# Hybrid decoder trunk: A's heads moved to the output projection, top-k rounds spread, side work ahead of weight splits, B turned a step earlier

## The chip, the cores and the metric

The kernel runs on one core of a Trainium2 chip. The metric is the device time of one execution in microseconds, given as the median of several runs.

## What is computed

Two layers of a decoder trunk, batch 1, 256 positions, model width 1024, all in float32:

```
h = h + 1/2 * SwiGLU_1(RMSNorm(h))
u = RMSNorm(h);  P = u @ W_in          # 3792 columns: A q,k,v | index q,k,w | B q,k,v | C q,k,v,f,g
o_A = sparse attention: 4 query heads, one shared key/value head; keys chosen per query by an
      indexer: score = sum_h w_h * relu(iq_h . ik), causal, the top 64 of 256
o_B = 4 heads; at 256 positions one block, so plain causal attention
o_C = 8 heads with a cumulative log-forget bias and a sigmoid gate
h = h + concat(o_A, o_B, o_C) @ W_out
h = h + 1/2 * SwiGLU_2(RMSNorm(h))
```

A and B use normalised and rotated queries and keys, C normalised ones.

## The kernel before

**Weights.** All large products run with the weights as two rounded halves (high and low), three matmuls for one (`mm3`). Each weight unit (128 x up to 1024) is split on the chip: ScalarE casts it to the high half (line 116), VectorE subtracts to get the low half (line 120). `W.take()` hands out the next unit; `W.pump()` queues one cast, and one subtraction for the unit before, as long as fewer than seven units are split ahead. There are eight buffers of split units and five raw 1 MB buffers, filled by SyncE's DMA queue.

**Order.** Every engine runs its instructions in the order in which the program issues them; there is no scheduler. Tiles rotate through pools: a new tile waits until the readers of the tile that had its place are done. PSUM has two rotating sets of four banks, `gu` and `acc`.

**The mixer.** First the input projection: eight chunks of columns (`CHUNKS`: iq, ib, b, a, ck, cq, cv, cg), four weight units each, so 32 steps. After each step the kernel issues `W.pump()`, counts the step and then issues the *side work* that is due (`at_step`, `run_side`): what has to be done to chunks that are there already, while TensorE goes on with the projections. After a chunk's fourth step its `post_` function evacuates its banks (two `gu` banks for each chunk). The side work, by step:

- 7 to 10: index queries and keys, stacked as high and low halves (`stack`, lines 605 and 606) and turned (`queries_T`, `keys_T`: matmuls with the identity into `acc` banks; ScalarE copies the high half, line 616 or 628, VectorE makes the low half of keys, line 629).
- 11 to 16: `index`: products, ReLU (ScalarE, line 717), weighted sum into `score` (VectorE, line 721).
- 13: `log_sigmoid` (ScalarE, with table loads), `bk_norm` (B's key norm; GpSimd writes the scaled keys twice, line 824). 14: `bq_split`.
- 16 to 23: `topk`, eight rounds that take out the eight largest of each row (VectorE, lines 739 and 741). 24: `amask`.
- 16: `cumsum`: matmul into an `acc` bank, which VectorE reads with four small copies (lines 763 and 764).
- `B_TURN` = 19: `bq_turn` and `bk_turn`, which take two `acc` banks each. From `B_STEP` = 20: B's heads by `run_heads`, one a step.
- 20: `a_norm`, `a_split`. `A_TURN` = 24: `a_turn`. From `A_STEP` = 25: A's heads.
- 21 and 25: C's sums of squares and norm.

`run_heads` makes five stages for a head: `scores` (TensorE; then VectorE scales, masks and takes the row's extreme, line 910), `exps` (ScalarE, lines 917 and 918), `flip` (three transposes, line 924, and a copy to SBUF, line 926; in the output projection by VectorE for even heads, ScalarE for odd ones), `values` (TensorE, then VectorE divides, line 940, and scales into `o`), and `outT` for each pair of heads (two transposes, line 957, then a high half by ScalarE, line 964, and a low half by VectorE, line 965).

**The output projection.** It runs into all four `acc` banks. `out_halves` issues the first five units (k-tiles of `W_out` in the order 2, 3, 0, 1, 4: B's two pairs, A's two, C's first) as ten halves of twelve matmuls, one half for each `next(halves)`, with a `W.pump()` behind each second half. C's eight heads run between the halves in the `gu` banks, software-pipelined: iteration i issues `scores(i)`, `flip(i - 1)`, `exps(i)`, a half, `values(i - 1)`. `c_T` turns two of C's heads (eight transposes, line 1024, two copies, line 1025). `tail` does the last three units, the residual and the next norm.

The two feed-forward blocks of a layer (`ffn`) are outside the change.

Of the kernel before, what the change touches and what calls it, by code (L numbers as in the profile page):

```python
# [35 lines left out]
DOWN_LAG = 4  # L36
OUT_TAIL = 3
WARM = 7
B_TURN, B_STEP, A_TURN, A_STEP = 19, 20, 24, 25


CHUNKS = [
# [9 lines left out]
OUT_ORDER = [2, 3, 0, 1, 4, 5, 6, 7]  # L52
# [88 lines left out]
def kernel(ctx: ExitStack, tc: tile.TileContext, x, ffn1_norm, ffn1_w_gate, ffn1_w_up, ffn1_w_down,  # L141
# [62 lines left out]
    W = Weights(tc, raw_pool, split_pool)  # L204
# [343 lines left out]
    def mixer(l, norm, nxt):  # L548
# [3 lines left out]
        def at_step(n, fn):  # L552
            side.append((n, next(count), fn))

        def run_side():
            due = sorted(x for x in side if x[0] <= step[0])
            for x in due:
                x[2]()
            side[:] = [x for x in side if x[0] > step[0]]
# [98 lines left out]
        def post_ib(ps):  # L658
# [92 lines left out]
                st["amask"] = am  # L751

            for r in range(TOPK // 8):
                at_step(16 + r, topk)
            at_step(24, amask)

            def cumsum():
                b = bank("acc")
# [8 lines left out]
        def post_a(ps):  # L767
            ss = sm.tile([P, 2, 5], F32, name="ssa", tag="ss")
            rot = [hp.tile([P, S], F32, name="aqr", tag="hl") for _ in range(2)]
            ak = [at.tile([P, 1, HD], F32, name=f"ak{t}", tag=f"ak{t}") for t in range(2)]  # L770
            akd = [at.tile([P, 2, HD], F32, name=f"akd{t}", tag=f"kd{t}") for t in range(2)]
            sq = []
            for t in range(2):
                evac(rot[t], ps[t][:, :256], t)
                evac(ak[t][:, 0], ps[t][:, 256:320], t)
                evac(va[t][:, 0, 0:64], ps[t][:, 320:384], t)
                sq.append(squares(ps[t][:, :320], t, 5))
                rope(heads(rot[t], 4), tab[:, 0, 0, t], tab[:, 0, 1, t])
                rope(ak[t], tab[:, 1, 0, t], tab[:, 1, 1, t])

            def a_norm():
                for t in range(2):
                    square_sums(ss[:, t], sq[t])
                rs = head_rs(ss.rearrange("p t h -> p (t h)"), 10, "a")
                for t in range(2):
                    scale_heads(akd[t], ak[t], rs[:, 5 * t + 4:5 * t + 5])
                st["ra"] = minus(rs, 10, "a")

            at_step(20, a_norm)

            def a_split():
                st["aq"] = [stack(x) for x in rot]

            def a_turn():
                st["aqT"] = at.tile([P, 4, S], F32R, name="aqT", tag="qs")
                st["akT"] = at.tile([P, 2, 1, S], F32R, name="akT", tag="ikT")
                queries_T(st["aqT"], st["aq"])
                keys_T(st["akT"], [d.rearrange("p a b -> p (a b)")[:, None] for d in akd])

            at_step(20, a_split)  # L800
            at_step(A_TURN, a_turn)

            def qk_a(h):
                return st["aqT"][:, h], [st["akT"][:, c, 0] for c in range(2)]

            run_heads([("A", h) for h in range(4)], qk_a, "acc", lambda i, fn: at_step(A_STEP + i, fn), 2)

        def post_b(ps):
            ss = sm.tile([P, 2, 4], F32, name="ssbk", tag="ss")
            rot = [hp.tile([P, S], F32, name="bkr", tag="hl") for _ in range(2)]  # L810
            sq = []
            for t in range(2):
                evac(rot[t], ps[t][:, :256], t)
                evac(va[t][:, 1:5, 0:64], heads(ps[t][:, 256:512], 4), t)
                sq.append(squares(ps[t][:, :256], t, 4))
                rope(heads(rot[t], 4), tab[:, 3, 0, t], tab[:, 3, 1, t])

            def bk_norm():
                for t in range(2):
                    square_sums(ss[:, t], sq[t])  # L820
                rs = head_rs(ss.rearrange("p t h -> p (t h)"), 8, "bk")
                for t in range(2):
                    twice = tmp(512).rearrange("p (h s d) -> p h s d", h=4, s=2)
                    G.tensor_tensor(twice, heads(rot[t], 4)[:, :, None, :].to_broadcast([P, 4, 2, HD]),
                                    rs[:, 4 * t:4 * t + 4, None, None].to_broadcast([P, 4, 2, HD]), op=ALU.mult)
                    bk.append(twice.rearrange("p h s d -> p h (s d)"))

            def bk_turn():
                st["bkT"] = at.tile([P, 2, 4, S], F32R, name="bkT", tag="kT")
                keys_T(st["bkT"], bk)  # L830

            bk = []
            at_step(13, bk_norm)
            at_step(B_TURN, bk_turn)

            def qk_b(h):
                return st["bqT"][:, h], [st["bkT"][:, c, h] for c in range(2)]

            run_heads([("B", h) for h in range(4)], qk_b, "acc", lambda i, fn: at_step(B_STEP + i, fn), 2)
# [48 lines left out]
        def run_heads(hs, qk, tag, emit=None, lag=1):  # L888
            pj, pt, op = {}, {}, {}

            def scores(i):

                kind, h = hs[i]
                q, k = qk(h)
                b = bank(tag)
                if kind == "C":
                    mm(b[:, 0:P], q[:, 0:P], k[:, 0:P], True, True)
                    mm(b[:, P:3 * P], q[:, P:S], k[:, 0:S], False, True)
                else:
                    products(b[:, 0:P], q[:, 0:P], [c[:, 0:P] for c in k], True, True)  # L900
                    products(b[:, P:3 * P], q[:, P:S], [c[:, 0:S] for c in k], False, True)
                mask = st["amask"] if kind == "A" else causal
                s = tmp(3 * P)
                nm = sm.tile([P, 2], F32, name="nm", tag="nm")
                for t, c in enumerate((slice(0, P), slice(P, 3 * P))):
                    scale = -1.0
                    if kind != "C":
                        col = (5 * t if kind == "A" else 4 * t) + h
                        scale = st["r" + kind.lower()][:, col:col + 1]
                    V.tensor_tensor_reduce(s[:, c], b[:, c], mask[:, c], scale, 3e38, op0=ALU.add, op1=ALU.min,  # L910
                                           accum_out=nm[:, t:t + 1])
                pj[i] = (s, nm)
# [66 lines left out]
        for name, cols in CHUNKS:  # L979
            n = sum(c[1] for c in cols)  # L980
            ps = [bank("gu") for _ in range(2)]
            for u in range(4):
                w = W.take()
                for kk in range(2):
                    k = 2 * u + kk
                    for t in range(2):
                        ts = slice(t * P, (t + 1) * P)
                        mm3(ps[t][:, :n], (norm.h[:, k, ts], norm.l[:, k, ts]), [v[:, kk] for v in w],
                            k == 0, k == KT - 1)
                if name == "iq" and u == 1:  # L990
                    norm.sums()
                W.pump(2 if name == "iq" else 1)
                step[0] += 1
                run_side()
            posts[name](ps)
        while side:
            step[0] += 1
# [21 lines left out]
        def c_T(hp_):  # L1019
            for d, src in zip(cT, (cqa, cka)):  # L1020
                b = bank("gu")
                for i in range(2):
                    for t in range(2):
                        T.transpose(b[:66, i * S + t * P:i * S + (t + 1) * P], src[t][:, 2 * hp_ + i, :], ident)  # L1024
                (A.copy if src is cqa else V.tensor_copy)(d[:66, 2 * hp_:2 * hp_ + 2],
                                                         b[:66].rearrange("p (a b) -> p a b", a=2))

        scores, exps, flip, values, outT = run_heads([("C", h) for h in range(8)],
                                                     lambda h: (cT[0][:66, h], cT[1][:66, h]), "gu")
        c_T(0)  # L1030
        next(halves)
        for i in range(9):
            if i < 8:
                scores(i)
            if i > 0:
                flip(i - 1)
            if i < 8:
                exps(i)
            if i > 0:
                next(halves)  # L1040
                values(i - 1)
                if i > 2 and i % 2:
                    outT((i - 3) // 2)
            if i in (0, 2, 4):
                c_T(1 + i // 2)
            if i == 0:
                next(halves)
        for _ in halves:
            raise AssertionError
        return tail(acc, oT, OUT_ORDER[8 - OUT_TAIL:], 1.0, nxt, lambda: outT(3))  # L1050


    def before_mixer(l):
# [119 lines left out]
```

## Time and profile before

| | us |
|---|---|
| median of 3 runs | 1066.82 |
| lowest to highest | 1066.6 to 1068.17 |
| the profiled execution | 1066.12 |
| its span, from the first to the last instruction | 1064.3 |

The profile is of one execution. A row of its timeline has the start and the length in us from the span's start, the engine (PE is TensorE, PEld its weight loads, DVE VectorE, ACT ScalarE, POOL GpSimd), the line of the kernel, the operation, what is written and read, the shapes and the number of merged instructions; in brackets the idle time before it and what ended that. TensorE's matmuls overlap, so the time that one costs is the distance between starts. Layer 0's mixer lies at about 198 to 350 us, layer 1's at about 724 to 877 us.

### The profile page before, as it was taken

Reading aid. Unit: us, or ns where it says so; the run is one execution under the profiler, and the core shown is the slowest. Engines: PE = TensorE matmul, PEld = TensorE weight load, DVE = VectorE, ACT = ScalarE, POOL = GpSimd, SP = SyncE. Lnnn points to the kernel's source line nnn. Section 1 sums busy time; section 2 is a strip of 40 time slices with the busy share of each in tenths; the row PEclk is TensorE's granted clock in tenths of the full one; section 3 lists DMA queues with packets and bytes.
Section 4 is the critical chain, followed back from the end, with each engine's and each line's share of the span. In section 5 each row is a group of like instructions: output and inputs, shape, how many; then the busy total and the mean of one; then the engine's idle time right before and its main releaser. Section 6 shows DMA issues by size and latency. Waiting matters only on the chain.

```text
span 1064.3 us, 16903 instructions
## 1 busy us (share of the span) xinstructions
PE 1049.6 (99%) x6611; PEld 950.2 (89%) x6611; DVE 827.4 (78%) x1564; ACT 595.8 (56%) x1022; POOL 160.6 (15%) x184
## 2 busy tenths in 40 slices
PE   9999999998999999999999999999989999999998
PEld 8999999997899899999989999999868998888887
DVE  6998777789856887777789777778897669877774
ACT  6565554676654565555456555547756455655551
POOL 2004000276400100000010300003765000000000
PEclk9999999999999999999999999999999999999999
DMA  9576465464332365564646565464544314564531
GB/s 324 203 240 205 157 231 158 135 222 159 120 118 81 119 237 175 182 207 149 199 159 219 175 208 184 172 185 165 173 148 155 119 41 147 210 234 155 205 119 40
DMA packets 130912, 181.81 MB, mean 171 GB/s; under 512 B 7008, under 2 KB 104720, under 8 KB 130832
## 3 DMA queue, kind: packets, MB, share of 16 engines
q1 hardware_dynamic: 130512, 180.65, 50.4%
q8 instruction: 52, 0.85, 0.3%
q14 instruction: 28, 0.23, 0.1%
q10 hardware_dynamic: 320, 0.08, 0.0%
HBM read 179.67 MB, written 1.05 MB: 170 GB/s over the span
## 4 chain that ended last, share of the span: by engine, by line
PE 59%; DVE 4%; ACT 1%; issue 1%; POOL 1%; POOLq 0%; ACTq 0%; DVEq 0%
PE ps_gu L293 38%; PE ps_acc L293 21%; DVE wl L120 1%; DVE score L721 1%; DVE score L741 0%; PE ps_gu L1024 0%; DVE m L739 0%; PE ps_gu L924 0%; DVE xhl L320 0%; PE ps_acc L924 0%; DVE hres L352 0%; DVE stacked L606 0%; ACT xhl L317 0%; POOL swapped L570 0%; PE ps_acc L383 0%
## 5 line engine op out<-in xcount | busy, mean ns | idle before, releaser
L120 DVE TENSOR_TENSOR wl<-raw,wh 128x1024 fp32r<-128x1024 f32 (+2 forms) x343 | 414.6, 1215 | 22.1 <-ACT wh L116 22.0
L293 PE MATMUL ps_gu<-xhl,wh 128*128 128x512 f32 (+1 forms) x1408 | 351.8, 391 | 0.2 <-DVE tmp L425 0.2
L116 ACT CAST wh<-raw 128x1024 fp32r<-128x1024 f32 (+2 forms) x343 | 345.1, 1035 | 4.0 <-PE ps_gu L293 2.0
L293 PEld LDWEIGHTS ps_gu<-xhl,wh 128*128 128x128 f32 x1408 | 253.6, 189 | 46.2 <-DVE tmp L425 0.4
L293 PEld LDWEIGHTS ps_gu<-xhl,wl 128*128 128x128 f32 x1400 | 192.0, 190 | 13.7
L293 PE MATMUL ps_gu<-xhl,wl 128*128 128x256 f32 x1400 | 198.0, 283 | 0.0
L293 PE MATMUL ps_gu<-wh,xhl 128*128 128x512 f32 (+2 forms) x512 | 162.4, 384 | 0.0
L425 DVE TENSOR_TENSOR tmp<-ps_gu,tmp 128x256 f32<-128x256 f32 x175 | 74.2, 424 | 105.8 <-ACT tmp L424 105.6
L293 PE MATMUL ps_acc<-hl,wh 128*128 128x256 f32 x528 | 149.7, 284 | 0.0
L293 PE MATMUL ps_acc<-hh,wl 128*128 128x256 f32 x528 | 149.4, 283 | 0.0
L293 PE MATMUL ps_acc<-hh,wh 128*128 128x256 f32 x528 | 149.4, 283 | 0.0
L424 ACT COPY tmp<-ps_gu 128x256 f32<-128x256 f32 x175 | 64.7, 370 | 132.7 <-PE ps_gu L293 127.0
L293 PEld LDWEIGHTS ps_gu<-wh,xhl 128*128 128x128 f32 x512 | 96.3, 191 | 14.8
L293 PEld LDWEIGHTS ps_acc<-hl,wh 128*128 128x128 f32 x528 | 101.4, 192 | 0.3
L293 PEld LDWEIGHTS ps_acc<-hh,wl 128*128 128x128 f32 x528 | 101.3, 192 | 0.0
L293 PEld LDWEIGHTS ps_acc<-hh,wh 128*128 128x128 f32 x528 | 101.3, 192 | 0.0
L293 PE MATMUL ps_gu<-wl,xhl 128*128 128x512 f32 (+2 forms) x256 | 96.8, 378 | 0.0
L331 POOL TENSOR_TENSOR ssacc<-ssacc,tmp 128x512 f32<-128x512 f32 x10 | 12.9, 1294 | 506.3 <-ACT tmp L329 327.7
L432 ACT ACTIVATE tmp<-tmp 128x256 f32<-128x256 f32 x88 | 36.8, 418 | 85.3 <-DVE tmp L430 85.3
L441 ACT CAST hh<-tmp 128x256 fp32r<-128x256 f32 x80 | 32.6, 407 | 86.5 <-DVE tmp L437 86.5
L293 PEld LDWEIGHTS ps_gu<-wl,xhl 128*128 128x128 f32 x256 | 49.0, 191 | 6.6
L430 DVE TENSOR_TENSOR tmp<-tmp,rb 128x256 f32<-128x256 f32 x88 | 37.7, 428 | 3.0
(246 smaller groups left out, 1229.9 us busy)
## 6 DMA issues: line engine op xcount, KB each, us to landing
raw<-in_ffn_w_down_dram SPq DMA_DIRECT2D x44, 1024.0 KB, 7.0
raw<-in_ffn_w_gate_dram SPq DMA_DIRECT2D x43, 1024.0 KB, 7.0
raw<-in_ffn_w_up_dram SPq DMA_DIRECT2D x43, 1024.0 KB, 5.2
raw<-in_w_in_dram SPq DMA_DIRECT2D x24, 1024.0 KB, 5.1
raw<-in_w_out_dram SPq DMA_DIRECT2D x8, 1024.0 KB, 4.9
raw<-in_w_in_dram SPq DMA_DIRECT2D x4, 768.0 KB, 5.2
raw<-in_w_in_dram SPq DMA_DIRECT2D x4, 656.0 KB, 4.6
xin<-in_x_dram SPq DMA_DIRECT2D x4, 256.0 KB, 5.2
```

What stands on the lines that cost most here:

```text
L116: self.nc.scalar.copy(hv, src)
L120: (engine or self.nc.vector).tensor_tensor(lv, self.srcs[self.n_low], hv.bitcast(F32), op=ALU.subtract)
L293: T.matmul(o, l, r, start=start, stop=stop, skip_group_check=True)
L331: G.tensor_tensor(self.acc, self.acc, sq, op=ALU.add)
L424: A.copy(o, ps[:, 1])
L425: V.tensor_tensor(o, ps[:, 0], o, op=ALU.add)
L430: V.tensor_tensor(t_, t_, norm.rb, op=ALU.mult)
L432: A.activation(th, t_, AF.Tanh, scale=0.5)
L441: (V.tensor_copy if late else A.copy)(hh, t_)
L721: V.scalar_tensor_tensor(sc, rl[:, i * n:(i + 1) * n], st["iw"][:, t, h:h + 1], st["cmask"][t] if first else sc, op0=ALU.mult, op1=ALU.add)
```

## The change

- A's four heads leave the side work. They become heads 0 to 3 of the list that runs among the halves of the output projection, ahead of C's eight: 13 iterations instead of 9, in the `gu` banks. The ten halves are placed as follows: one ahead of the loop, one in each iteration but 3, 5, 9 and 12. `c_T` runs in iterations 3, 5, 7 and 9 (before: one ahead of the loop, then 0, 2 and 4).
- The eight top-k rounds are due at steps 17, 19, ... 31, and `amask` at 32.
- `B_TURN` is 18 in place of 19; B's heads still start at step 20.
- `a_norm` is due at 22, `a_split` at 24, `a_turn` at 26.
- In each step of the input projection the side work is issued ahead of `W.pump()`, not behind it.

```diff
-B_TURN, B_STEP, A_TURN, A_STEP = 19, 20, 24, 25
+B_TURN, B_STEP, A_ROOT, A_TURN = 18, 20, 22, 26
...
-                at_step(16 + r, topk)
-            at_step(24, amask)
+                at_step(17 + 2 * r, topk)
+            at_step(32, amask)
...
-            at_step(20, a_norm)
+            at_step(A_ROOT, a_norm)
...
-            at_step(20, a_split)
+            at_step(A_TURN - 2, a_split)
             at_step(A_TURN, a_turn)
 
-            def qk_a(h):
-                return st["aqT"][:, h], [st["akT"][:, c, 0] for c in range(2)]
-
-            run_heads([("A", h) for h in range(4)], qk_a, "acc", lambda i, fn: at_step(A_STEP + i, fn), 2)
...
-                W.pump(2 if name == "iq" else 1)
                 step[0] += 1
                 run_side()
+                W.pump(2 if name == "iq" else 1)
             posts[name](ps)
...
-        scores, exps, flip, values, outT = run_heads([("C", h) for h in range(8)],
-                                                     lambda h: (cT[0][:66, h], cT[1][:66, h]), "gu")
-        c_T(0)
+        def qk_ac(kind, h):
+            if kind == "A":
+                return st["aqT"][:, h], [st["akT"][:, c, 0] for c in range(2)]
+            return cT[0][:66, h], cT[1][:66, h]
+
+        hs = [("A", h) for h in range(4)] + [("C", h) for h in range(8)]
+        scores, exps, flip, values, outT = run_heads(hs, qk_ac, "gu")
+        n = len(hs)
         next(halves)
-        for i in range(9):
-            if i < 8:
+        for i in range(n + 1):
+            if i < n:
                 scores(i)
             if i > 0:
                 flip(i - 1)
-            if i < 8:
+            if i < n:
                 exps(i)
+            if i in (3, 5, 7, 9):
+                c_T((i - 3) // 2)
+            if i not in (3, 5, 9, n):
+                next(halves)
             if i > 0:
-                next(halves)
                 values(i - 1)
                 if i > 2 and i % 2:
                     outT((i - 3) // 2)
-            if i in (0, 2, 4):
-                c_T(1 + i // 2)
-            if i == 0:
-                next(halves)
...
-        return tail(acc, oT, OUT_ORDER[8 - OUT_TAIL:], 1.0, nxt, lambda: outT(3))
+        return tail(acc, oT, OUT_ORDER[8 - OUT_TAIL:], 1.0, nxt, lambda: outT(n // 2 - 1))
```

More of the change, by code (lines that the diff above doesn't have):

```diff
@@ L834, in post_b, with qk_b @@
             at_step(B_TURN, bk_turn)
-            def qk_b(h):
+            def qk_b(kind, h):
                 return st["bqT"][:, h], [st["bkT"][:, c, h] for c in range(2)]
@@ L893, in scores @@
                 kind, h = hs[i]
-                q, k = qk(h)
+                q, k = qk(kind, h)
                 b = bank(tag)
```

## The prediction

> **What bounds the kernel now.** I read the page's busy shares first, then TensorE's waits, then the timeline around the longest wait, engine by engine.
>
> ```profile
> PE 1049.6 (99%) x6611; PEld 950.2 (89%) x6611; DVE 827.4 (78%) x1564; ACT 595.8 (56%) x1022; POOL 160.6 (15%) x184
> ```
>
> TensorE is the limit, and the change leaves its matmuls as they are. So a gain can only come out of TensorE's idle time and slow stretches, and a loss only from new ones. TensorE's waits name where they are:
>
> ```profile
> PE ps_acc L293 <- DVE bkT L629: 8.3, 2, 4.1
> ```
>
> Two waits of 4.1 us, one in each layer's mixer, on VectorE's low half of B's turned keys (`keys_T`, line 629). The other waits of TensorE are 1 us or less. The place in layer 0 (the work of step 19, then step 20, then B's first scores, then step 21):
>
> ```profile
> 250.71 1.00 PE L293 MATMUL ps_acc<-identr,stacked 128*128 128x128 f32 x8
> 251.56 1.23 PE L626 MATMUL ps_acc<-cst,tmp 128*128 128x128 f32 x8
> 252.54 0.48 PE L293 MATMUL ps_gu<-wh,xhl 128*128 128x512 f32 x1
> ```
>
> ```profile
> 255.39 0.22 PE L293 MATMUL ps_acc<-bkT,bqT 128*128 128x128 f32 x1
> 259.75 0.76 PE L293 MATMUL ps_acc<-bkT,bqT 128*128 128x128 f32 x3 [4.13 <-DVE bkT L629]
> 260.30 0.63 PE L293 MATMUL ps_gu<-wh,xhl 128*128 128x512 f32 x1
> ```
>
> ```profile
> 264.54 0.62 PE L293 MATMUL ps_acc<-bkT,bqT 128*128 128x128 f32 x4
> 265.00 0.39 PE L293 MATMUL ps_gu<-wh,xhl 128*128 128x512 f32 x1
> ```
>
> Undisturbed, one B score takes 265.00 - 264.54 = 0.46 us and a step of projections behind side work 255.39 - 252.54 = 2.85 us. From 255.39 to 264.54 stand one of each, 3.31 us, and 9.15 us went by: 5.84 us lost, more than the wait. The rest is the clock:
>
> ```profile
> 253.23:256.64 3.41, 2.38 (x12) 1.74 (x10) 3.41 (x14) 1.13 (x2) 3.25 (x5) 1.00 0.14 37
> 256.64:260.06 3.42, 0.31 (x2) 0.31 (x3) 3.42 (x9) 0.00 (x0) 2.23 (x5) 1.00 0.85 302
> 260.06:263.47 3.41, 3.41 (x11) 2.74 (x10) 3.41 (x13) 1.74 (x5) 0.00 (x0) 0.50 0.26 49
> ```
>
> The columns are busy us of PE, PEld, DVE, ACT and POOL, then the granted clock. After a stretch in which TensorE was busy for 0.31 us, the next 3.41 us ran at clock 0.50; after one with 1.03 us idle (2.38 of 3.41 busy) the clock stayed 1.00. Layer 1 is the same:
>
> ```profile
> 781.76 0.22 PE L293 MATMUL ps_acc<-bkT,bqT 128*128 128x128 f32 x1
> ```
>
> ```profile
> 790.69 0.62 PE L293 MATMUL ps_acc<-bkT,bqT 128*128 128x128 f32 x4
> ```
>
> 8.93 us for 3.31: 5.62 us lost. Together 11.46 us are to be had.
>
> VectorE is the late one: it ran without a gap from here
>
> ```profile
> 239.56 0.48 DVE L721 SCALAR_TENSOR_TENSOR score<-tmp,iw,causal 128x256 f32<-128x256 f32 x1 [1.29 <-ACT tmp L717]
> ```
>
> to the keys' low half, and step 16's last index product, made at 241.63, was scored at 248.97:
>
> ```profile
> 241.63 0.63 PE L293 MATMUL ps_acc<-ikT,iqT 128*128 128x256 f32 x4
> ```
>
> ```profile
> 248.97 1.56 DVE L721 SCALAR_TENSOR_TENSOR score<-tmp,iw,score 128x256 f32<-128x256 f32 x2
> 250.46 0.61 DVE L739 MAX8 m<-score 128x8 f32<-128x128 f32 x2
> ```
>
> ```profile
> 251.64 0.15 DVE L763 COPY cqa<-ps_acc 128x8 f32<-128x8 f32 x1
> ...
> 251.93 1.21 DVE L120 TENSOR_TENSOR wl<-raw,wh 128x1024 fp32r<-128x1024 f32 x1
> ```
>
> ```profile
> 259.02 1.27 DVE L629 TENSOR_TENSOR bkT<-ps_acc,bkT 128x512 fp32r<-128x512 f32 x2
> ```
>
> A top-k round is 251.64 - 250.46 = 1.18 us, the cumulative sum's four copies about 0.3, a low split about 1.2.
>
> **The change part by part.** *B turned at step 18, rounds spread.* ScalarE gates the restart at 239.56: VectorE waits there for its ReLU, which stands behind the log-sigmoid's table loads. In the changed order one weight cast that stood between B's evacuations and that chain goes behind it, and the one of the step before goes ahead of the evacuations: the same number of casts ahead of the chain, so I keep 239.56. From there to the end of the scores (250.46) VectorE's order is unchanged. Then the cumulative sum's copies come at once, without the round ahead of them: done at 250.46 + 0.37 = 250.83. Then a split (1.2), one round (1.18), a split (1.2), the keys (1.2): ready at 255.6, not 260.2; four rounds before the keys become one, six splits five.
>
> TensorE now turns B one step earlier. Three steps lie between 242.46 and 250.71, so 2.75 each:
>
> ```profile
> 242.46 0.48 PE L293 MATMUL ps_gu<-wh,xhl 128*128 128x512 f32 x1
> ```
>
> The turn starts at 250.71 - 2.75 = 247.96. Its keys need GpSimd's doubled keys, ready in time at 244.16 + 3.20 = 247.36:
>
> ```profile
> 244.16 3.20 POOL L824 TENSOR_TENSOR tmp<-bkr,y_bk 128x512 f32<-128x512 f32 x2
> ```
>
> But the turn takes four accumulator banks of four, and the last is the one that the cumulative sum's copies read. That wait is already there, small: the fifth key transpose, due 251.56 + 4 x 0.11 = 252.0, came at
>
> ```profile
> 252.16 0.30 PE L626 MATMUL ps_acc<-cst,tmp 128*128 128x128 f32 x1
> ```
>
> 0.15 us after the last copy. After the change TensorE is there at 247.96 + 0.85 + 0.44 = 249.25 and the copies end at 250.83, so it goes on at about 250.95: **a new wait of 1.7 us** in place of 0.15, or +1.55. Behind it: TensorE needs the keys after step 20, at 250.95 + 0.5 + 2.75 + 2.85 = 257.05, and they are ready at 255.6. So the 4.1 us wait goes, with 1.4 us to spare, and with it the half clock.
>
> Can 1.7 us of idleness halve the clock? The rows bound it: 1.03 idle did not, 3.1 did; 1.7 is nearer the first, so I take no loss, with a rival below. The Trainium skill (TensorE: Matmul & The Clock Gate, "What's actually happening") has half rate come after an idle window of some 3.4 us, which a 1.7 us wait cannot fill; by that rule too the sum stays. The trace agrees only loosely, as the window ahead of the half clock still held 0.31 us of work.
>
> *Side work ahead of splits.* The first turn of the index queries waited for a stacked low half behind a split, in both layers, and took 0.39 us longer than the second:
>
> ```profile
> 219.31 1.39 PE L293 MATMUL ps_acc<-identr,stacked 128*128 128x128 f32 x8
> ```
>
> ```profile
> 745.53 1.39 PE L293 MATMUL ps_acc<-identr,stacked 128*128 128x128 f32 x8
> ```
>
> ```profile
> 223.37 1.00 PE L293 MATMUL ps_acc<-identr,stacked 128*128 128x128 f32 x8
> ```
>
> ```profile
> 218.78 0.87 DVE L606 TENSOR_TENSOR stacked<-iqr,stacked 128x256 fp32r<-128x256 f32 x2
> ```
>
> A split now stands behind these two, so they end about 1 us earlier: -0.39 per layer. ScalarE's casts queue behind its ReLUs, which wait for TensorE; weights are split up to seven units ahead, so a step's delay there reaches nobody.
>
> *A's heads moved.* TensorE's work for them is the same. A step of projections behind side work costs 2.85, one without 2.75; steps with side work of TensorE that a projection follows fall from 13 (19 to 31) to 9: -0.4 per layer. A's norm and turn (22, 24, 26) only have to be done by step 32.
>
> *Output projection.* There are 13 iterations for ten halves of 1.5 us, so four (3, 5, 9 and the last, 12) have none. In 3, 5 and 9 the value product waits for VectorE's copy of the turned probabilities. The row of before: scores end at 313.97, the copy ends at 314.73 + 0.55 = 315.28,
>
> ```profile
> 313.97 0.49 PE L924 MATMUL ps_gu<-cst,p 128*128 128x128 f32 x3
> ```
>
> ```profile
> 314.73 0.55 DVE L926 COPY pT<-ps_gu 128x384 f32<-128x384 f32 x1
> ```
>
> 1.31 later, 1.4 with the release. TensorE then has the flip (0.24) and `c_T` (four and four transposes, 0.44 each) to do, 1.12:
>
> ```profile
> 319.43 0.60 PE L1024 MATMUL ps_gu<-cst,cqa 128*66 128x128 f32 x4
> 319.87 0.60 PE L1024 MATMUL ps_gu<-cst,cka 128*66 128x128 f32 x4
> ```
>
> 0.3 us of waiting, three times: +0.9. In the last iteration nothing stands between flip and values:
>
> ```profile
> 337.06 0.49 PE L924 MATMUL ps_gu<-cst,p 128*128 128x128 f32 x3
> 337.30 0.36 PE L293 MATMUL ps_acc<-oh,wh 128*128 128x256 f32 x1
> ```
>
> ```profile
> 337.64 0.48 ACT L926 COPY pT<-ps_gu 128x384 f32<-128x384 f32 x1
> ```
>
> The copy ends at 338.12, so values start at 338.2, 0.9 after the flip: +0.9. Elsewhere a half covers the chain.
>
> **The sum.** Layer 0: -5.84 - 0.39 - 0.4 + 1.55 + 0.9 + 0.9 = -3.28. Layer 1: -5.62 and the same others: -3.06. Together -6.3. The profiled execution took 1066.12 (span 1064.3), the median of the runs is 1066.82, 0.7 above it. I predict against the median: 1066.82 - 6.3 = **1060.5 us**.
>
> **The rivals.**
> 1. *The new wait halves the clock.* Idle of 1.7 lies between the 1.03 and 3.1 of the rows, so it can. Of layer 0's 5.84 us, 260.30 - 255.39 - 0.46 = 4.45 is the wait and 1.4 the clock; twice 1.4: 1063.3. Chance 0.11.
> 2. *The bank wait is not there*, because the copies come sooner: -3.4 more, 1057.1. Against it: the same release gap stands in both layers. Chance 0.07.
> 3. *The 4.1 us wait shortens only*: VectorE is later than I have it by over 1.4 us (two scores that take 1 us took 2.4 while GpSimd doubled the keys). At 4 us later, 2.6 us of waiting come back per layer: 1065.7, no change. Chance 0.06.
> 4. *Slower: VectorE late at the seam.* Four rounds and A's mask now stand in steps 25 to 32, ahead of A's first scores. TensorE reaches A's first flip one half and one score (1.97 us) after the scores, and the chain to it needs about 1.45, so a lag over 0.5 us stalls it. A lag of 7 us is on record at step 16. With 4 us, 3.5 of waiting and 1.4 of clock per layer: 1070.3. It turns into a loss from a lag of about 2.3. Against it is the load there:
>
> ```profile
> 280.00:296.00 16.00, 16.00 (x96) 14.05 (x95) 9.86 (x31) 9.99 (x20) 13.68 (x7) 1.00 0.48 157
> 296.00:308.00 12.00, 12.00 (x68) 10.19 (x68) 6.47 (x13) 6.60 (x10) 0.00 (x0) 1.00 0.30 90
> 308.00:345.00 37.00, 37.00 (x311) 36.17 (x310) 24.50 (x79) 18.20 (x38) 0.00 (x0) 1.00 0.27 86
> ```
>
> VectorE was busy for 9.9 of 16 us and 6.5 of 12, with A's softmax in it; four rounds add 4.7 to the 28 us. Chance 0.06.
> 5. *Transposes leave the clock idle.* Iterations 3, 5 and 9 hold 1.3 us of transposes and 0.3 of waiting in about 2.4 us. If transposes count as idle, each could halve one stretch, at most 1.7 us, six times: 1070.7, slower. Against it, `c_T` and flips stood in 308 to 345 at clock 1.00. Chance 0.03. The Trainium skill (same page, "Part 4: PE-mode transpose") says that transposes do not count as busy in the same way.
>
> **How the numbers follow.** My forecast has 0.64, the rivals 0.33, and 0.03 is left to others. Its own spread is 1058.5 to 1063, as its small terms are each uncertain by half. The range of 1057.0 to 1065.0 takes in the first two rivals; the seam, the transposes and most of rival 3 lie outside. About 0.2% (2.1 us) is what a measurement of this kernel can tell from no change. Faster: the forecast, rivals 1 and 2 and part of 3, 0.86; same 0.06; slower 0.08.
>
> **What would show it.** In the changed profile TensorE's wait for bkT is gone and a wait of 1 to 2.5 us stands among B's key transposes, released by the copies of line 763; clock 1.00 throughout both mixers; waits of 0.2 to 0.5 us ahead of three value products and near 0.9 ahead of the last; A's first flip not late. A wait for the mask or at B's first scores, or a stretch at 0.50, proves me wrong.

## The result, and the profile after

The changed kernel takes **1060.86 us** (median of four runs, 1060.17 to 1061.7) against 1066.94 beside it (four runs, 1066.6 to 1068.17): ratio 0.9941, 95% interval 0.9924 to 0.9958, some 6.1 us less. The profiled execution of the changed kernel took 1061.49 us, with a span of 1059.7. In its profile the line numbers behind `run_heads` are four lower: scores L906, exponentials L913 and L914, flip L920, the copy `pT` L922, `c_T` L1020.

The page's busy shares, and TensorE's waits (us in total, times, longest):

```profile
PE 1049.7 (99%) x6611; PEld 950.5 (90%) x6611; DVE 829.2 (78%) x1568; ACT 594.1 (56%) x1018; POOL 164.1 (15%) x184
```

```profile
PE ps_acc L626 <- DVE cka L764: 3.2, 2, 1.6
PE ps_gu L293 <- ACT pT L922: 1.2, 2, 0.6
PE ps_gu L293 <- POOL minus_half L182: 1.0, 1, 1.0
```

TensorE's busy time is what it was (1049.6). The two waits of 4.1 us for bkT are gone; in their place stand two of 1.6 us for the copies of the cumulative sum (line 764), and one of 0.6 us in each layer for the last turned probabilities. The place in layer 0, TensorE's timeline:

```profile
247.51 1.00 PE L293 MATMUL ps_acc<-identr,stacked 128*128 128x128 f32 x8
248.35 0.62 PE L626 MATMUL ps_acc<-cst,tmp 128*128 128x128 f32 x4
250.60 0.63 PE L626 MATMUL ps_acc<-cst,tmp 128*128 128x128 f32 x4 [1.63 <-DVE cka L764]
250.99 0.48 PE L293 MATMUL ps_gu<-wh,xhl 128*128 128x512 f32 x1
...
256.52 0.62 PE L293 MATMUL ps_acc<-bkT,bqT 128*128 128x128 f32 x4
```

and VectorE's beside it:

```profile
248.62 1.54 DVE L721 SCALAR_TENSOR_TENSOR score<-tmp,iw,score 128x256 f32<-128x256 f32 x2
250.08 0.16 DVE L763 COPY cqa<-ps_acc 128x8 f32<-128x8 f32 x1
...
250.30 0.16 DVE L764 TENSOR_SCALAR cka<-ps_acc 128x8 f32<-128x8 f32 x1
...
251.75 0.61 DVE L739 MAX8 m<-score 128x8 f32<-128x128 f32 x2
...
254.06 1.27 DVE L629 TENSOR_TENSOR bkT<-ps_acc,bkT 128x512 fp32r<-128x512 f32 x2
```

The last index score is followed at once by the copies; they end at 250.46 and TensorE's fifth key transpose starts at 250.60. The keys are ready at 255.33, and B's first scores start at 256.52 without a wait: 1.2 us to spare.

The granted clock there, in windows (busy us of PE, PEld, DVE, ACT, POOL, then the clock); the first two are layer 0, the others layer 1:

```profile
248.73:252.15 3.42, 1.79 (x12) 1.41 (x11) 3.38 (x9) 1.82 (x4) 3.26 (x5) 1.00 0.19 72
252.15:255.56 3.41, 3.41 (x17) 2.83 (x16) 3.41 (x9) 1.61 (x2) 3.18 (x5) 1.00 0.74 225
...
770.97:774.39 3.42, 1.81 (x18) 1.60 (x17) 3.38 (x8) 2.00 (x4) 3.26 (x4) 1.00 0.48 185
774.39:777.80 3.41, 3.41 (x11) 2.63 (x10) 3.41 (x9) 2.48 (x3) 3.25 (x6) 0.50 0.41 114
```

The same wait left the clock at 1.00 in layer 0 and took half of it for 3.41 us in layer 1. The four runs show it as well: mean clock 1.000 at 1060.17 and 1060.22 us, 0.998 at 1061.49 and 1061.70. One such stretch costs about 1.4 us here.

The output projection: iteration 5, without a half between `c_T` and the value product, and the last flip.

```profile
313.07 0.60 PE L1020 MATMUL ps_gu<-cst,cqa 128*66 128x128 f32 x4
313.51 0.60 PE L1020 MATMUL ps_gu<-cst,cka 128*66 128x128 f32 x4
314.11 0.88 PE L293 MATMUL ps_gu<-va,pT 128*128 128x65 f32 x6
...
334.66 0.49 PE L920 MATMUL ps_gu<-cst,p 128*128 128x128 f32 x3
335.77 0.88 PE L293 MATMUL ps_gu<-va,pT 128*128 128x65 f32 x6 [0.62 <-ACT pT L922]
```

From the keys' turns to the values 0.60 us go by (0.73 and 0.60 in iterations 3 and 9). Undisturbed it is 0.36 where a half follows (iteration 7 of layer 1), and 0.43 where a value product follows without waiting (iteration 2 of experiment 5). From the last flip to its values 1.11 go by, in place of 0.25 from a flip to a half.

### The profile page after: what moved, and what is told of

Same layout as the page of the kernel before. It is cut to its first block, busy times and chain, and to the rows that moved or that the text cites. A ratio compares the mean times of both kernels' runs of the same rounds, so it can differ in the third digit from the quotient of the medians.

```text
span 1059.7 us, 16913 instructions
## 1 busy us (share of the span) xinstructions
PE 1049.7 (99%) x6611; PEld 950.5 (90%) x6611; DVE 829.2 (78%) x1568; ACT 594.1 (56%) x1018; POOL 164.1 (15%) x184
## 4 chain that ended last, share of the span: by engine, by line
PE 62%; DVE 2%; ACT 1%; issue 1%; POOL 0%; POOLq 0%; ACTq 0%; DVEq 0%
PE ps_gu L293 41%; PE ps_acc L293 20%; DVE score L721 0%; PE ps_gu L920 0%; PE ps_gu L1020 0%; DVE wl L120 0%; DVE xhl L320 0%; DVE hres L352 0%; ACT xhl L317 0%; PE ps_acc L383 0%; ACT tmp L329 0%; POOLq L1169 0%; POOL y_n L304 0%; PE ps_gu L953 0%; PE ps_acc L920 0%
## 5 line engine op out<-in xcount | busy, mean ns | idle before, releaser
L293 PE MATMUL ps_gu<-wh,xhl 128*128 128x512 f32 (+2 forms) x512 | 159.5, 382 | 0.0
```

The costliest lines, as they stand in the source:

```text
L293: T.matmul(o, l, r, start=start, stop=stop, skip_group_check=True)
```

## The experiments

The forecast's theory: VectorE's order ahead of B's keys was the whole limit; the loss that is left is the bank wait (1.6 us a layer, plus a half clock at times) and four iterations without cover (1.7 us a layer). The rival: VectorE is behind through all of B's part, so a wait that is taken away at one place comes up at the next. Diffs are against the changed kernel unless said otherwise; every ratio is against the kernel before, on the same chip.

**1. The heads moved alone.** Against the kernel *before*: only A's heads go to the output projection, with the changed placing of halves and `c_T`; rounds, steps and queue order stay.

> The kernel before with one part of the change: A's heads run ahead of C's in the output projection, in the changed loop; rounds, steps and the order of splits as before. Theory (moving the heads gains nothing by itself, it only makes room for the rounds): the 4.1 us waits for bkT and their half clock stay, four fewer steps pay 0.1 us each, the output projection pays 1.7 us per layer: 1066.9 + 2 x 1.3 = 1069.5 us. Rival (taking A's softmax off VectorE in the projections is what frees it): the wait for bkT shrinks, below 1066 us.

Measured 1071.27 us, ratio 1.0044 (1.0032 to 1.0057). Its waits:

```profile
PE ps_acc L293 <- DVE bkT L629: 8.3, 2, 4.1
PE ps_gu L293 <- ACT pT L922: 1.2, 2, 0.6
```

The wait for bkT keeps its 4.1 us, so the rival is out: moving the heads is a loss by itself, the terms of the output projection. It is 1.8 us larger than expected. A part of that is the clock, which in this profile was at 0.50 for two stretches behind each 4.1 us wait, not one as in the profile of before (mean clock 0.994 in all five runs, 0.995 or 0.997 in those of before):

```profile
255.09:258.51 3.42, 0.32 (x3) 0.07 (x1) 3.42 (x14) 0.00 (x0) 3.19 (x5) 1.00 0.63 192
258.51:261.92 3.41, 2.37 (x7) 2.08 (x8) 3.41 (x9) 0.39 (x1) 0.32 (x1) 0.50 0.30 120
261.92:265.33 3.41, 3.41 (x9) 2.64 (x9) 3.38 (x12) 3.41 (x9) 1.18 (x1) 0.50 0.90 300
```

**2. Dense rounds.**

```diff
-                at_step(17 + 2 * r, topk)
+                at_step(16 + r, topk)
```

> The changed kernel with the eight top-k rounds at steps 16 to 23 again, one a step. Theory: the cumulative sum's copies come one round (1.18 us) later, so the wait among the key transposes is 2.8 us in place of 1.6; three rounds stand ahead of the keys' low half in place of one, which is ready at about 257.6 when TensorE needs it at about 257.7, so no second wait; 2.8 us idle of a 3.41 us window halve the clock in both layers: 1060.2 + 2.4 + 2.8 = 1065.4 us. Rival (the earlier turn alone makes the gain, the spread of the rounds nothing): 1061 us.

Measured 1066.33, ratio 0.9997 (0.9988 to 1.0006): with eight dense rounds nothing is left of the gain.

```profile
PE ps_acc L626 <- DVE cka L764: 5.6, 2, 2.8
```

```profile
250.34 0.61 DVE L739 MAX8 m<-score 128x8 f32<-128x128 f32 x2
...
251.51 0.16 DVE L763 COPY cqa<-ps_acc 128x8 f32<-128x8 f32 x1
```

A round again stands ahead of the copies, which makes the bank wait 1.2 us longer, and the clock halved in both layers. So the gain hangs on keeping the first round behind the copies. That the rounds behind it have to be spread isn't shown: there was no second wait here, for the keys, and eight rounds one step apart from step 17 on were not run. An estimate from the changed kernel's rows: one more round ahead of the keys (1.18 us) would use up the 1.2 us that they have to spare.

**3. B turned at 19.** `B_TURN` 18 to 19.

> The changed kernel with B turned at step 19 again. Theory: the copies of the cumulative sum are done before the turn gets to its fourth bank, so that wait (1.6 us) goes; the keys stand behind one more split and one more round, ready at about 257.6, and TensorE needs them at 254.9: 2.8 us of waiting for bkT per layer, and the clock halves behind it: 1060.2 + 2.1 + 2.8 = 1065 us; with the clock kept, 1062.3. Rival (the turn's place makes no difference now that the rounds are spread): 1060 us or, with the bank wait gone, 1057.

Measured 1062.62, ratio 0.9966 (0.9954 to 0.9979).

```profile
PE ps_acc L293 <- DVE bkT L629: 4.4, 2, 2.2
```

The bank wait is gone and the wait for the keys is back, at 2.2 us for 4.1 (2.8 expected). The profiled execution has a halved stretch in both layers, as has one other run by its mean clock (0.997, at 1063.63 and 1064.23 us); the other three, at 1062.31 to 1062.62, have a mean clock of 0.998, one such stretch. One step earlier is worth about 1.8 us: it trades 2.2 us for 1.6 in each layer, and the changed kernel had one halved stretch in two of its four runs, where this one has one or two in each.

**4. Weight splits ahead of the side work again.**

```diff
+                W.pump(2 if name == "iq" else 1)
                 step[0] += 1
                 run_side()
-                W.pump(2 if name == "iq" else 1)
```

> The changed kernel with each step's weight split ahead of its side work again. Theory: the number of splits ahead of the cumulative sum's copies and of the keys stays the same, so the wait among the key transposes keeps its 1.6 us; only the first turn of the index queries waits again, 0.39 us per layer: 1060.2 + 0.8 = 1061.0 us. Rival (the order within a step is what brings the keys in time): a wait at B's first scores comes back, at least 1.2 us per layer, 1063 us or more.

Measured 1060.46, ratio 0.9941 (0.9928 to 0.9955): no difference from the change that can be told. The first turn of the index queries is slow again,

```profile
220.99 1.39 PE L293 MATMUL ps_acc<-identr,stacked 128*128 128x128 f32 x8
222.22 0.45 PE L293 MATMUL ps_gu<-wh,xhl 128*128 128x512 f32 x1
```

1.23 us, where the changed kernel takes 0.84 (219.21 to 220.05), so the forecast's term of 0.39 is there. (This execution, 1063.78 us, is the slowest of the five: it was 1.7 us behind the changed kernel's profile already ahead of the mixer, and it has one halved stretch. The other four took 1060.13 to 1060.56 at full clock.) The bank wait fell from 1.6 to 1.5 us, which gives a part of it back:

```profile
PE ps_acc L626 <- DVE cka L764: 3.0, 2, 1.5
```

The rest is below what these runs resolve.

**5. Halves spread evenly.**

```diff
-            if i in (3, 5, 7, 9):
-                c_T((i - 3) // 2)
-            if i not in (3, 5, 9, n):
+            if i in (2, 4, 6, 8):
+                c_T((i - 2) // 2)
+            else:
                 next(halves)
```

> The changed kernel with c_T in iterations 2, 4, 6 and 8 of the output projection in place of 3, 5, 7 and 9, and a half in every iteration but those four, the last one included. Theory (a value product waits where no half covers the copy of the turned probabilities; VectorE's copy is the slow one, behind the row extremes, and c_T covers ScalarE's): the waits of 0.25 to 0.4 us ahead of three value products and the one of 0.8 us ahead of the last go, about 0.05 comes back four times: -1.5 us per layer, 1060.2 - 3.0 = 1057.2 us. Rival (the value products wait because VectorE is loaded there, whatever stands between): 1060 us, with waits of the same size in other iterations.

Measured 1057.38, ratio 0.991 (0.9896 to 0.9923). The wait of the last values is gone:

```profile
PE ps_acc L626 <- DVE cka L764: 3.2, 2, 1.6
...
PE ps_gu L1020 <- ACT pT L922: 0.4, 2, 0.2
```

Even heads' probabilities are copied by VectorE, odd ones by ScalarE; a half now covers every flip of an even head and the last flip (of head 11), and `c_T` alone covers those of heads 1, 3, 5 and 7. Against the change's runs without a half clock (1060.2) that is 2.8 us, 1.4 a layer; the terms it attacks were 0.85 and 0.86 a layer (as counted below), and 0.2 a layer comes back inside `c_T`.

**6. The cumulative sum later, with the change's halves and with even ones.** `at_step(16, cumsum)` to 19, so that its bank isn't the one the keys need.

> The changed kernel with the cumulative sum due at step 19, behind B's turn, so that its bank is no longer one of the four that the turn takes. Theory (the 1.6 us wait among B's key transposes is the bank that the cumulative sum's copies read; the keys themselves are nearly in time): that wait goes in both layers, TensorE reaches B's first scores 1.7 us earlier, at about 254.8 of layer 0, and the keys' low half ends at about 255.0, so 0 to 0.3 us of waiting for bkT take its place: 1060.2 - 3.2 = 1057.0 us, clock 1.00 throughout. Rival (VectorE is simply late, and the bank only shows it): the wait moves to bkT and keeps its size, 1060 us.

> The changed kernel with both edits: the cumulative sum at step 19 and c_T in the even iterations with a half in all others. Theory (two separate waits on TensorE's path): the gains add up, 1060.2 - 3.2 - 3.0 = 1054.0 us. Rival (a stretch that starts earlier meets the next late engine): half of the second gain is lost, 1055.5 us.

Measured 1062.65, ratio 0.996 (0.9948 to 0.9973), and with even halves 1059.32, ratio 0.9932 (0.9919 to 0.9944): both about 2 us *worse* than without the move. About 1.4 of these 2 us is a halved stretch: nine of the ten runs have a mean clock of 0.998 or less, and the one at 1.000 (with even halves) took 1057.81, as against 1057.38 without the move. The bank wait went, and the theory with it:

```profile
PE ps_acc L293 <- ACT pT L922: 4.0, 2, 2.0
```

This is B's first value product, in both layers of both kernels. Its row on TensorE, and ScalarE's timeline, with the sum later and the change's halves:

```profile
267.46 0.88 PE L293 MATMUL ps_acc<-va,pT 128*128 128x65 f32 x6 [2.01 <-ACT pT L922]
...
264.55 1.05 ACT L116 CAST wh<-raw 128x1024 fp32r<-128x1024 f32 x1
266.21 0.40 ACT L913 ACTIVATE p<-tmp,nm 128x128 f32<-128x128 f32 x1 [0.62 <-DVE nm L906]
266.54 0.51 ACT L914 ACTIVATE p<-tmp,nm 128x256 f32<-128x256 f32 x1
266.95 0.46 ACT L922 COPY pT<-ps_acc 128x384 f32<-128x384 f32 x1
```

The copy that TensorE needs stands behind the exponentials of head 2, and these wait for VectorE's reduction of head 2's scores, which VectorE reaches late. The rival was right in kind: the bank wait had hidden a lateness further on.

**7. The cumulative sum earlier.** Even halves and `at_step(15, cumsum)`: the copies come ahead of the last index scores. Is it the copies' place, or VectorE's lateness whatever their place?

> The changed kernel with the halves in the even iterations and the cumulative sum at step 15 in place of 16, so that its bank's four copies come ahead of the last index scores on VectorE. VectorE's work up to the keys is the same, only its order differs. Theory (the wait on the bank hid a backlog that comes up later whatever the copies' place): the 1.6 us wait at the key transposes goes, TensorE comes 1.6 us sooner to B's first value product and waits there 1.6 to 2.0 us: 1057.0 to 1059.5. Rival: the later place of the copies at step 19 was what made VectorE late for B, so with early copies the gain stays: 1057.4 - 3.2 = 1054.2.

Measured 1057.95, ratio 0.9922 (0.9907 to 0.9936), not below the 1057.38 of experiment 5.

```profile
PE ps_acc L293 <- ACT pT L922: 3.5, 2, 1.7
```

The bank wait is gone again, and 1.7 us stand at the same value product. The two runs with a mean clock of 1.000 and 0.999 took 1057.24 and 1057.34, as in experiment 5; the two with 0.998, one halved stretch, took 1058.57 and 1058.95. The copies' place isn't the cause.

**8. Flip first.** Experiment 6 with even halves, and in `run_heads`:

```diff
-                emit(i + lag, lambda i=i: flip(i))
+                emit(i + lag - 0.6, lambda i=i: flip(i))
```

A flip and its copy are then issued ahead of the scores and exponentials of the same step.

> The changed kernel with the halves in the even iterations, the cumulative sum at step 19, and each of B's flips issued ahead of the scores of the same step and not behind them. In the two kernels with the cumulative sum at step 19 TensorE lost 2.0 us in each layer at B's first value product. Theory: the copy of the turned probabilities (0.46 us) only stood in the wrong place in ScalarE's queue, behind the exponentials of head 2, which wait for VectorE's late reduction; ahead of them the copy can run right behind ScalarE's weight cast (ended at 265.3 in the layer's time, TensorE gets to the value product at about 265.2), so 0.4 to 0.6 us of the 2.0 stay: 1057.4 - 3.2 + 2 x 0.5 = 1055.2, with no half clock. Rival: VectorE's backlog itself is the limit, and the wait shows up at the next thing that needs VectorE (a flip or a value product of head 2 or 3): 1057.4 or more.

Measured **1054.68 us** (1054.48 to 1056.05), ratio 0.989 (0.9873 to 0.9906), the fastest of all.

```profile
PE ps_acc L293 <- ACT pT L922: 0.5, 2, 0.3
```

```profile
265.81 1.06 ACT L116 CAST wh<-raw 128x1024 fp32r<-128x1024 f32 x1
266.74 0.49 ACT L922 COPY pT<-ps_acc 128x384 f32<-128x384 f32 x1
267.45 0.40 ACT L913 ACTIVATE p<-tmp,nm 128x128 f32<-128x128 f32 x1 [0.21 <-DVE nm L906]
```

The copy now runs right behind the cast, and ScalarE waits for VectorE behind it, where nobody is delayed. VectorE's lateness was real but not the bound; the queue order on ScalarE passed it on to TensorE. The flip's move was run only together with the later sum; by itself it should leave the bank wait, which stands earlier in TensorE's queue, but no run shows that.

**9. Do transposes leave the clock idle?** At step 30, 64 extra matmuls of 128x128 whose results nobody reads: transposes in layer 0 (line 772), plain products with the identity in layer 1.

> The changed kernel with 64 extra matmuls of 128 x 128 at step 30, whose results nobody reads: in layer 0 transposes of the identity, in layer 1 plain products of the rounded identity with itself. One look at the granted clock behind them. Theory (the gate counts TensorE's idle time alone): both run back to back for 3.5 to 7 us and no stretch behind them is at clock 0.50. Rival (transposes do not count as work for the gate): in layer 0 the clock goes to 0.50 within or right behind the filler, in layer 1 it stays at 1.00; the transposes then take 0.22 us each in the halved stretch.

One execution, 1077.43 us. The transposes filled 294.54 to 301.7, so all of the second window here, and all of the clock's own stretch from 297.18 to 300.60 (counted on by 3.41 us from the halved one below):

```profile
293.40:297.00 3.60, 3.60 (x29) 3.35 (x28) 3.60 (x9) 1.26 (x2) 0.00 (x0) 1.00 0.96 305
297.00:300.40 3.40, 3.40 (x33) 3.40 (x32) 2.97 (x7) 0.00 (x0) 0.00 (x0) 1.00 0.84 285
```

A stretch of 3.41 us with transposes alone did not lower the clock, nor did the plain products. Apart from the kernel's last 3 us, the clock was halved once, behind the bank wait of layer 0:

```profile
249.40:252.81 3.41, 1.78 (x17) 1.57 (x16) 3.37 (x8) 1.97 (x4) 3.25 (x4) 1.00 0.52 201
252.81:256.23 3.42, 3.42 (x11) 2.65 (x10) 3.42 (x9) 2.48 (x3) 3.26 (x6) 0.50 0.42 108
```

## Why the prediction was right, point by point

- *The 4.1 us wait goes.* Right, with its times: scores ending at about 250.1 (250.46 predicted), copies done at 250.46 (250.83), keys at 255.33 (255.6), 1.2 us to spare (1.4).
- *A new wait of 1.7 us on the cumulative sum's bank.* Right: 1.63 and 1.61. From the turn's start to the next projection 3.48 us go by (250.99 - 247.51) against 1.83 before (252.54 - 250.71): +1.65 for a predicted +1.55.
- *The index queries' first turn, -0.39.* Right: 0.84 us. Experiment 4 shows that it brings less in the total than in its row.
- *Uncovered iterations, 0.9 and 0.9.* Right in size: 0.37 + 0.24 + 0.24 = 0.85, and 0.86. With 0.43 as the undisturbed spacing the first is 0.64. They were taken as the price of the change; experiment 5 shows that eight tenths of it was only the halves' placing.
- *Fewer steps with side work, -0.4.* Not isolated by any run. With the other terms as measured, layer 0 is -5.84 - 0.39 + 1.65 + 0.85 + 0.86 = -2.87 and layer 1 -2.65, together -5.5; with the term, -6.3. In the profiles, from the first projection of layer 0's mixer to the first product behind the mixer (197.77 to 348.33 before, 197.72 to 345.38 after), 2.90 us went, which is the sum without the term. Against the profiled execution of before, 1066.12, from which the terms were read, the runs without a half clock lie 5.9 us lower, between the two sums.
- *The base, 0.7 above the profiled execution.* The prediction adds it without a reason. The runs of before that have a mean clock on record show one: 21 of 31 have 0.995, about three halved stretches, and nine 0.997, the two that the profiled execution had. So the median run had more half clock to lose than the sum counts, while the sum's 6.3 is 0.4 more than came off the profiled execution. These two misses have opposite signs and largely cancel, which is luck.
- *No half clock, with rival 1 beside it.* Here the text was too sure in both directions: it bounded the effect by idle time alone and set it for both layers or none. In the profiled execution it came in one, in two of the four runs in none. A stretch at 0.50 was the prediction's own sign of being wrong, and it came up in two runs of four: this step, that the clock is kept, held in the other two alone. The measured median lies between the two kinds of run (1060.2 and 1061.6), which is part of why 1060.5 and 1060.86 agree; that is luck too.
- *Rival 4, VectorE late at the seam.* Not seen: A's first flip in the output projection starts with no wait,

```profile
300.71 0.49 PE L920 MATMUL ps_gu<-cst,p 128*128 128x128 f32 x3
```

- *Rival 5, transposes.* Ruled out by experiment 9 at the length tried: 64 in a row. So the sentence of the Trainium skill (TensorE: Matmul & The Clock Gate, "Part 4: PE-mode transpose") that transposes don't count as busy in the same way isn't borne out here, as far as holding a full clock goes. Whether transposes alone bring a halved clock back up was not run.
- *What the prediction did not see*: VectorE is late beyond the keys too. In the changed kernel the bank wait holds TensorE back by enough to hide it; experiments 6 and 7 uncover it.

## What to carry to other kernels

A wait that is taken away shows the next late engine on the same path: follow the queue of the engine that releases, and look for an instruction that somebody needs behind one that waits for somebody else; moving the producer alone (the cumulative sum) gained nothing here, and with that copy moved ahead as well (the flip's) the gain came. Work that is taken from one stage into another is paid there; spread the filler of that stage evenly over the new iterations before the price is accepted. A short idle time has no fixed price: a granted clock per stretch, in several runs, belongs to its reading.

## What the runs showed of the hardware

The clock is granted in stretches of 3.41 us (a halved row is 3.41 or 6.83 us long), which lie elsewhere against the work in each execution. TensorE's waits of 1.5 to 2.0 us in these profiles halved the next stretch in 6 cases of 14; the longer ones (2.2, 2.8, 4.1 us) in all 8. In three of the eight harmless cases, each a 2.0 or 1.7 us wait, the border of two stretches fell inside the wait. In the others the wait lay within one stretch as in the harmful ones; equal idle time then had both outcomes (1.79 and 1.81 us busy in the profile after). The columns streamed in the stretch (the widths of the matmuls that start in it, added up from the timeline) order the cases better: in the profile after they are 3,072 in layer 0 and 2,304 in layer 1. With up to 2,560 of them the next stretch was halved, but for one case with 2,176 (experiment 4, layer 1; two others with that sum were halved); from 2,688 on, entered at full clock, it was not. No run varied these columns by themselves, so it remains an ordering of these cases and not a shown cause. The Trainium skill (TensorE: Matmul & The Clock Gate, "What's actually happening") asks for an idle window of some 3.4 us before half rate; here 1.5 us of idleness in a stretch (experiment 4, layer 0) was enough in some executions, and the measurement decides.
